# Where the last head's pooling is handed out, which queue loads the padded grids, and where sixteen modulation rows are computed

## The chip, the cores and the metric

The kernel runs on one core of a Trainium2 chip. The metric is the device time of one execution in microseconds (us); of several executions the median is taken. A core has a matrix engine (TensorE, PE in the profile), VectorE (DVE), ScalarE (ACT), GpSimd (POOL) and SyncE (SP), each with an instruction stream of its own; they wait for each other by semaphores. Transfers between device memory and the core's memory (SBUF) are started by an instruction in the stream of SP or POOL and carried by sixteen DMA engines. A load is "handed out" where the program asks for it, and it "lands" when its data is there.

## The reference, cut to what matters

One layer over 512 latent tokens and 256 context tokens of width 1024, in fp32. A combined input projection feeds a pooling mixer and a four-head mLSTM; a gated sum of the two goes through the output projection, and an FFN of width 2816 follows. The layer is modulated by six vectors of 1024 that are computed from `c` (`mod = silu(c) @ w_ada + b_ada`). What the change touches is the pooling mixer and the last four of these six vectors:

```python
mod = jax.nn.silu(c) @ w_ada[l] + b_ada[l]
sh1, sc1, g1, sh2, sc2, g2 = jnp.split(mod[:, None, :], 6, axis=-1)
...
for g, w in enumerate(POOL_WINDOWS):                 # windows 2, 4, 8, 16
    ug = uf[..., g * G:(g + 1) * G]                  # 256 channels of each group
    ug2 = ug.reshape(B, rows, GRID_W, G)             # 8 rows of 64 tokens
    s_r, cnt_r = _window_sum(ug2, w, 1)
    s_rc, cnt_c = _window_sum(s_r, w, 2)
    mean = (s_rc / (cnt_r[:, None] * cnt_c[None, :])[None, :, :, None]).reshape(B, N, G)
    outs.append(jnp.einsum('bnc,cd->bnd', (mean - ug).astype(u.dtype), w_pool[g]))
...
y = jax.nn.sigmoid(p[5]) * pool_out + jax.nn.sigmoid(p[6]) * m_out
return y @ w_out
```

## The kernel before, in words

Channels lie on the 128 partitions, tokens along the free dimension, so a tile of 128 channels by 512 tokens is the unit of work. Every fp32 operand is split into a high and a low part, ACT rounding the high part and DVE subtracting for the low part, and every product is three matmuls (`mm3`, lines 188 to 190: high by high, high by low, low by high). `wload` (L153 to L157) loads a weight strip, ACT makes `wh` (L156), DVE makes `wl` (L157). `split` (L177, L178) does the same for any tile, so `pm` at L177 is the high part and at L178 the low part of a pooled tile, and `act` that of an input of the output projection.

**The stage of pairs.** The pooling input and its gate are projected by a Strassen scheme, eight weight pairs, class `Seven` with the subclass `Pool`. `prepare` loads two strips of a pair (L224 `ur`, L225 `wr`), and makes its sums and splits on ACT and DVE; one low part per strip comes by an accumulating load on POOL's queue (L236, 128 rows of 2 KB; the first of the stage starts at 76.4 us, the last at 149.2 us). `Pool.later` (L852) stores the gate and calls `late_mod(2, ...)`, `Pool.done` stores the pooling input `ud[j]` to device memory.

**Modulation rows.** `late` runs over the 32 blocks of the last four modulation vectors. `late_mod(n, behind, among)` (L676) takes the next `n`: a load of 512 KB (L683) and one DVE instruction (L685) that multiplies by `silu(c)` and sums along the row. Among the pairs the load goes to the `wr` buffers (three, shared with the weight strips), else to the `pb` buffers (two, shared with the pooling). Sixteen are taken among the pairs, two for each pair, and sixteen behind the scores of the attention.

**Heads.** `for h in range(H)` (about L1075): attention of head `h`; queries and keys of head `h+1`; `both_pooled(h)`; `values(h+1)`; and `mixed(h, pp)`, which multiplies the two pooled tiles by `wpool` and combines them with the head's output. `pooled(j)` sets the grid buffer `pa` to zero on POOL (L617), loads `ud[j]` into its middle (L618: 128 partitions, 8 rows of 256 bytes in each, from SP), sums over rows and columns on DVE (L624 or L629, then L634), loads the reciprocal window sizes (L637), multiplies (L641) and subtracts (L642), and splits into `pm`. There is one `pa` buffer: the next tile's zeroing waits for L642 of the tile before. In the last head there are no next keys and values; in their place the six finished tiles of the mixer's output (`yd`) are loaded again by SP (`y_split`, L1048) and split into `act`, and the output projection starts on them. There `rest()` turns the last half of the head's output by transposes (L1013).

Outside two blocks of manual order a list scheduler puts the instructions of each engine in order. It goes by the order in which the program hands them out and by the tiles' dependencies, so a call that is moved in the program moves instructions of other work too.

## Time and profile before

| | |
|---|---|
| time, median of 3 runs (lowest, highest) | 902.58 us (902.25, 903.84) |
| profiled execution, own time | 906.13 us |
| profiled execution, span from first to last instruction | 904.4 us |
| mean granted TensorE clock | 0.992 |
| PE busy | 880.4 us, 97% of the span |
| DVE, ACT, POOL busy | 640.7 us, 474.1 us, 78.9 us |
| DMA, mean over the span | 149 GB/s |

A row of the waits reads: engine, tile and line that waited, "<-" and what ended the wait, then us in total, times, longest. A row of the timeline reads: start, duration, engine, line, operation, tiles, and in brackets how long the engine had been idle before it and what ended that. "xN" are N instructions of a kind put together. A row of the windows gives the busy time of PE, PEld, DVE, ACT and POOL with their instructions, the granted clock, the share of the sixteen DMA engines, and GB/s.

### The profile page before, as it was taken

How to read it: one execution, taken by the hardware profiler on the slowest of the kernel's cores; microseconds unless marked ns; L12 is line 12 of the kernel's file. 1: busy time of each engine (PE TensorE's matmuls, PEld its weight loads, DVE VectorE, ACT ScalarE, POOL GpSimd, SP SyncE). 2: the span in 40 equal slices, each digit the busy share in tenths (PEclk: the TensorE clock that was granted, in tenths of full speed). 3: DMA queues.
4: the chain of work that ended last, by engine and by line, in shares of the span. 5: the costliest groups of instructions: out<-in, count | busy, mean ns of one | idle time of the engine just before them, and what ended most of it. 6: DMA issues, size and time to landing. Idle time of an engine off the chain costs nothing. (4 is left out here: it accounts for less than half of the span.)

```text
span 904.4 us, 15980 instructions
## 1 busy us (share of the span) xinstructions
PE 880.4 (97%) x6218; PEld 810.7 (90%) x6218; DVE 640.7 (71%) x1243; ACT 474.1 (52%) x919; POOL 78.9 (9%) x109
## 2 busy tenths in 40 slices
PE   9999999999999999999999899999999999999997
PEld 8679999879897989989887699999889998899997
DVE  4699896679667867877687667885366754867644
ACT  4576564456536454635364348574145741666542
POOL 0001111000001001100100000020011100111000
PEclk9999999999999999999999899999999999999999
DMA  9838999723126313712436550385356643766402
GB/s 353 307 119 214 281 329 254 266 60 110 55 82 198 107 59 105 223 44 73 150 119 197 196 180 22 81 215 126 93 159 150 146 118 87 203 142 132 127 1 94
DMA packets 56397, 135.12 MB, mean 149 GB/s; under 512 B 13536, under 2 KB 17920, under 8 KB 55296
## 3 DMA queue, kind: packets, MB, share of 16 engines
q1 hardware_dynamic: 48544, 119.93, 40.7%
q0 software_dynamic: 7776, 14.16, 9.5%
q8 instruction: 49, 0.80, 0.4%
q14 instruction: 28, 0.23, 0.1%
HBM read 125.40 MB, written 8.67 MB: 148 GB/s over the span
## 5 line engine op out<-in xcount | busy, mean ns | idle before, releaser
L157 DVE TENSOR_TENSOR wl<-wr,wh 128x1024 fp32r<-128x1024 f32 (+3 forms) x62 | 72.8, 1175 | 34.3 <-ACT wh L156 33.6
L156 ACT CAST wh<-wr 128x1024 fp32r<-128x1024 f32 (+3 forms) x62 | 61.8, 1000 | 64.5 <-PE ps L189 47.2
L188 PE MATMUL ps<-a,wh 128*128 128x512 f32 (+1 forms) x240 | 88.8, 370 | 0.0
L189 PE MATMUL ps<-a,wh 128*128 128x512 f32 (+1 forms) x240 | 88.7, 370 | 0.0
L190 PE MATMUL ps<-a,wl 128*128 128x512 f32 (+1 forms) x240 | 88.6, 369 | 0.0
L188 PE MATMUL ps<-act,wh 128*128 128x512 f32 (+1 forms) x224 | 78.7, 351 | 1.9 <-ACT wh L156 1.8
L190 PE MATMUL ps<-act,wl 128*128 128x512 f32 (+1 forms) x224 | 78.4, 350 | 0.9 <-DVE wl L157 0.9
L189 PE MATMUL ps<-act,wh 128*128 128x512 f32 (+1 forms) x224 | 78.2, 349 | 0.0
L177 ACT CAST wh<-sg 128x1024 fp32r<-128x1024 f32 x27 | 28.4, 1051 | 56.4 <-PE pat L189 46.0
L723 PE MATMUL ps<-wl,a 128*128 128x256 f32 (+1 forms) x192 | 54.4, 284 | 0.9 <-DVE wl L157 0.9
L236 POOL DMA_DIRECT2D ol<-in_wffi x38 | 32.9, 873 | 256.4 <-ACT ol L235 86.9
L722 PE MATMUL ps<-wh,a 128*128 128x256 f32 (+1 forms) x192 | 54.3, 284 | 0.0
L724 PE MATMUL ps<-wh,a 128*128 128x256 f32 (+1 forms) x192 | 54.3, 283 | 0.0
L190 PEld LDWEIGHTS ps<-a,wl 128*128 128x128 f32 x240 | 45.2, 189 | 7.2
L1336 DVE SCALAR_TENSOR_TENSOR x<-ps,lb,x 128x512 f32<-128x512 f32 (+1 forms) x32 | 19.6, 616 | 45.2 <-PE ps L190 45.2
L178 DVE TENSOR_TENSOR wl<-sg,wh 128x1024 fp32r<-128x1024 f32 x27 | 33.0, 1224 | 26.0 <-ACT wh L177 25.8
L189 PEld LDWEIGHTS ps<-a,wh 128*128 128x128 f32 x240 | 45.3, 189 | 6.9
L188 PEld LDWEIGHTS ps<-a,wh 128*128 128x128 f32 x240 | 45.3, 189 | 6.8
L188 PE MATMUL ps<-hp,gh 128*128 128x256 f32 x176 | 50.2, 285 | 1.0 <-ACT pat L272 1.0
L188 PEld LDWEIGHTS ps<-act,wh 128*128 128x128 f32 x224 | 42.7, 191 | 7.9 <-ACT wh L156 2.3
L188 PE MATMUL ps<-hp,oh 128*128 128x256 f32 x176 | 49.2, 279 | 0.1
L190 PE MATMUL ps<-hp,gl 128*128 128x256 f32 x176 | 49.1, 279 | 0.0
(365 smaller groups left out, 3023.4 us busy)
## 6 DMA issues: line engine op xcount, KB each, us to landing
wr<-in_w SPq DMA_DIRECT2D x34, 512.0 KB, 4.7
wr<-in_wffi SPq DMA_DIRECT2D x25, 512.0 KB, 4.2
ur<-in_wffi SPq DMA_DIRECT2D x19, 512.0 KB, 4.2
ol<-in_wffi POOLq DMA_DIRECT2D x38, 256.0 KB, 5.2
ada<-in_wada_a SPq DMA_DIRECT2D x8, 1024.0 KB, 8.7
wr<-in_wada_b SPq DMA_DIRECT2D x16, 512.0 KB, 5.7
pb<-in_wada_b SPq DMA_DIRECT2D x16, 512.0 KB, 4.7
wr<-in_wffo SPq DMA_DIRECT2D x16, 448.0 KB, 3.7
```

Source lines behind the costliest of these rows:

```text
L156: nc.scalar.copy(wh, raw[:, :n])
L157: V.tensor_sub(wl, raw[:, :n], wh.bitcast(F32))
L177: nc.scalar.copy(h, src)
L178: low_part[0] = V.tensor_sub(l, src, h.bitcast(F32))
L188: nc.tensor.matmul(dst, wh, ah, start=first and i == 0, stop=False, skip_group_check=on)
L189: nc.tensor.matmul(dst, wh, al, start=False, stop=False, skip_group_check=on)
L190: nc.tensor.matmul(dst, wl, ah, start=False, stop=last and i == n - 1, skip_group_check=on)
L236: nc.gpsimd.dma_start(l, dram, accum_op=ALU.add)
L722: nc.tensor.matmul(acc[:, :n], ah, wh, start=kk == 0, stop=False)
L723: nc.tensor.matmul(acc[:, :n], ah, wl, start=False, stop=False)
L724: nc.tensor.matmul(acc[:, :n], al, wh, start=False, stop=kk == KT - 1)
L1336: V.scalar_tensor_tensor(x1[j][:, c], acc[:, c], g2[:, j:j + 1], x1[j][:, c], ALU.mult, ALU.add)
```

## The change

Four edits, made together. `pooled` issues the grid load from POOL's stream, right behind its zeroing. The reciprocals are loaded once in `both_pooled(h)` and shared by the head's two tiles, four loads in place of eight. In the last head `both_pooled(h)` is called ahead of the six `y_split(j)`. And `Pool.later` takes one modulation row for an even pair and two for an odd one, 12 in all; the four that are left go to the end of `values(1)` and `values(2)`, which are handed out in the passes of head 0 and head 1, two each, with loads into `pb`.

```diff
--- before.py
+++ after.py
@@ -598,7 +598,7 @@
         return ks
 
 
-    def pooled(j):
+    def pooled(j, ic):
 
         w = (2, 4, 8, 16)[j // 2]
         R, W0 = 8, 64
@@ -615,7 +615,7 @@
         n = R + rl + rr
         A = view(tl("pa", [P, PBW]), n, wid)
         nc.gpsimd.memset(A, 0.0)
-        nc.sync.dma_start(A[:, rl:rl + R, lw:lw + W0], ud[j].rearrange("p (r c) -> p r c", r=R))
+        nc.gpsimd.dma_start(A[:, rl:rl + R, lw:lw + W0], ud[j].rearrange("p (r c) -> p r c", r=R))
         steps = [1] + [2 ** (i + 1) for i in range({2: 0, 4: 1, 8: 2, 16: 3}[w])]
         cur = A
         if w <= 8:
@@ -633,8 +633,6 @@
             B = pb(n, cw - st)
             V.tensor_add(B, cur[:, :, 0:cw - st], cur[:, :, st:cw])
             cur, cw = B, cw - st
-        ic = S("tmp")
-        nc.sync.dma_start(ic, icnt[j // 2:j // 2 + 1, :].broadcast_to([P, T]))
         mean = S("tmp")
         m3 = mean.rearrange("p (r c) -> p r c", r=R)
         i3 = ic.rearrange("p (r c) -> p r c", r=R)
@@ -730,7 +728,9 @@
                 for d, j in ((0, i), (1, 1 - i if i < 2 else 7 - i)):
                     V.tensor_add(gif[:, :, d, j, :], gsrc[:, d], bsrc[:, d])
             nc.scalar.copy(vh[:, i, :DH], acc[:, :DH])
-            V.tensor_sub(vl[:, i, :DH], acc[:, :DH], vh[:, i, :DH].bitcast(F32))
+            low = V.tensor_sub(vl[:, i, :DH], acc[:, :DH], vh[:, i, :DH].bitcast(F32))
+            if 0 < h < H - 1 and i in (0, 1):
+                late_mod(1, low)
         return vh, vl
 
 
@@ -852,7 +852,7 @@
         def later(self, j, s, y, q):
             tanh_half(s[:, TC:], y)
             nc.sync.dma_start(td[j], s)
-            late_mod(2, self.sub, True)
+            late_mod(1 + j % 2, self.sub, True)
 
         def done(self, j, s, x, q):
             nc.scalar.copy(q[:, :TC], x)
@@ -1059,7 +1059,9 @@
         return t
 
     def both_pooled(h):
-        return [pooled(2 * h + e) for e in range(2)]
+        ic = S("tmp")
+        nc.sync.dma_start(ic, icnt[h:h + 1, :].broadcast_to([P, T]))
+        return [pooled(2 * h + e, ic) for e in range(2)]
 
     def mixed(h, pp):
         yb = pool_mix(h, pp)
@@ -1085,9 +1087,9 @@
             for n in ("att", "kqp", "vg"):
                 close_pool(n)
             open_pool("late1", ("act", "oh", "ol", "gh", "gl"))
+            pp = both_pooled(h)
             for j in range(6):
                 y_split(j)
-            pp = both_pooled(h)
             mgate_all(KT - 1)
             rest()
         mixed(h, pp)
```

The places that the prediction speaks of, as the instruction streams stand before and after. The edits shift the line numbers: L681, L639, L640, L651 and L663 after are L683, L641, L642, L653 and L665 before.

**SP in the stage of pairs.** `wr_...<-in_wada_b` is the load of a modulation row, `wr` and `ur` `<-in_w` are the strips of a pair. Before, the loads of the first pairs:

```order
L683 DMA wr_1201<-in_wada_b 128x1024
L224 DMA ur_1236<-in_w 128x1024
L683 DMA wr_1204<-in_wada_b 128x1024
L225 DMA wr_1235<-in_w 128x1024
L854 DMA td<-tmp_1101 128x512
L224 DMA ur_1368<-in_w 128x1024
L859 DMA ud<-tmp_1074 128x512
L683 DMA wr_1333<-in_wada_b 128x1024
L683 DMA wr_1336<-in_wada_b 128x1024
L225 DMA wr_1367<-in_w 128x1024
```

After:

```order
L681 DMA wr_1201<-in_wada_b 128x1024
L224 DMA ur_1233<-in_w 128x1024
L225 DMA wr_1232<-in_w 128x1024
L681 DMA wr_1330<-in_wada_b 128x1024
L854 DMA td<-tmp_1101 128x512
L224 DMA ur_1365<-in_w 128x1024
L859 DMA ud<-tmp_1074 128x512
L681 DMA wr_1333<-in_wada_b 128x1024
L225 DMA wr_1364<-in_w 128x1024
```

Ahead of the strip `wr` of a pair there stood two modulation rows and now there is one.

**POOL at the end of head 0.** `pa` are the grids of head 0's second tile and of head 1's first, L900 are the decay masks of head 1. Before:

```order
L1004 TENSOR_TENSOR rst_2393<-ss_2392,mhalf 128x2
L617 MEMSET pa_3092 128x585
L617 MEMSET pa_4013 128x737
L900 TENSOR_TENSOR tmp_3332<-E_3331,maskF 128x256
L900 TENSOR_TENSOR tmp_3332<-E_3331,maskB 128x256
L900 TENSOR_TENSOR tmp_3427<-E_3426,maskF 128x256
L900 TENSOR_TENSOR tmp_3427<-E_3426,maskB 128x256
```

After:

```order
L1004 TENSOR_TENSOR rst_2381<-ss_2380,mhalf 128x2
L617 MEMSET pa_3080 128x585
L618 DMA pa_3080<-ud 128x8x64
L617 MEMSET pa_4007 128x737
L618 DMA pa_4007<-ud 128x8x64
L900 TENSOR_TENSOR tmp_3324<-E_3323,maskF 128x256
L900 TENSOR_TENSOR tmp_3324<-E_3323,maskB 128x256
L900 TENSOR_TENSOR tmp_3419<-E_3418,maskF 128x256
L900 TENSOR_TENSOR tmp_3419<-E_3418,maskB 128x256
```

Each zeroing now has its load behind it in the same stream, and the masks stand behind both.

**DVE in the last head.** `pa`, `pb`, `pm` belong to the two pooled tiles (grids of 128x316 and smaller), `act` are the low parts of the six loaded tiles, `wl` 128x1024 that of a strip of the output projection. Before:

```order
L178 TENSOR_TENSOR act_5693<-tmp_5690,act_5692 128x512
L641 TENSOR_TENSOR tmp_5721<-pb_5717,tmp_5719 128x512
L178 TENSOR_TENSOR act_5699<-tmp_5696,act_5698 128x512
L642 TENSOR_TENSOR tmp_5721<-tmp_5721,pa_5702 128x512
L157 TENSOR_TENSOR wl_5904<-wr_5901,wh_5903 128x1024
L178 TENSOR_TENSOR pm_5725<-tmp_5721,pm_5724 128x512
L1037 TENSOR_TENSOR m_5335<-m_5335,m_5221 128x512
L629 TENSOR_TENSOR pb_5731<-pa_5728 128x316
L629 TENSOR_TENSOR pb_5733<-pb_5731 128x158
L629 TENSOR_TENSOR pb_5735<-pb_5733 128x79
L634 TENSOR_TENSOR pb_5737<-pb_5735 128x78
L634 TENSOR_TENSOR pb_5739<-pb_5737 128x76
```

After, from the second tile's column sums on:

```order
L634 TENSOR_TENSOR pb_5695<-pb_5693 128x78
L634 TENSOR_TENSOR pb_5697<-pb_5695 128x76
L634 TENSOR_TENSOR pb_5699<-pb_5697 128x72
L634 TENSOR_TENSOR pb_5701<-pb_5699 128x64
L157 TENSOR_TENSOR wl_5896<-wr_5893,wh_5895 128x1024
L639 TENSOR_TENSOR tmp_5703<-pb_5701,tmp_5660 128x512
L1037 TENSOR_TENSOR m_5329<-m_5329,m_5215 128x512
L640 TENSOR_TENSOR tmp_5703<-tmp_5703,pa_5686 128x512
L178 TENSOR_TENSOR pm_5707<-tmp_5703,pm_5706 128x512
L178 TENSOR_TENSOR act_5713<-tmp_5710,act_5712 128x512
L178 TENSOR_TENSOR act_5719<-tmp_5716,act_5718 128x512
L98 SCALAR_TENSOR_TENSOR m_5746<-tmp_5780,m_5746 128x512
```

The splits of `act` stood ahead of both `pm` and around the first; now both `pm` come first, and the strip's `wl` stands between the second tile's column sums and its multiplication.

**ACT in the last head.** The names are the same; `wh` 128x1024 and `gh` are strips of the output projection, L653 (L651 after) scales the pooled product. Before:

```order
L177 CAST act_5698<-tmp_5696 128x512
L156 CAST wh_5903<-wr_5901 128x1024
L177 CAST pm_5724<-tmp_5721 128x512
L1015 ACTIVATE m_5221<-pat_5822,quarter_mg 128x256
L1015 ACTIVATE m_5222<-pat_5822,quarter_mg 128x256
L177 CAST gh_5952<-wr_5950 128x1024
L177 CAST gh_5958<-wr_5956 128x1024
L94 ACTIVATE tmp_5788<-ps_5789 128x512
L177 CAST pm_5750<-tmp_5747 128x512
L653 ACTIVATE tmp_5842<-ps_5835,half_ps 128x512
L653 ACTIVATE tmp_5851<-ps_5844,half_ps 128x512
L156 CAST wh_5928<-wr_5926 128x1024
```

After:

```order
L177 CAST pm_5682<-tmp_5679 128x512
L177 CAST gh_5944<-wr_5942 128x1024
L156 CAST wh_5895<-wr_5893 128x1024
L1015 ACTIVATE m_5215<-pat_5814,quarter_mg 128x256
L1015 ACTIVATE m_5216<-pat_5814,quarter_mg 128x256
L177 CAST pm_5706<-tmp_5703 128x512
L177 CAST act_5712<-tmp_5710 128x512
L177 CAST act_5718<-tmp_5716 128x512
L94 ACTIVATE tmp_5780<-ps_5781 128x512
L177 CAST act_5724<-tmp_5722 128x512
L651 ACTIVATE tmp_5834<-ps_5827,half_ps 128x512
L177 CAST act_5730<-tmp_5728 128x512
```

The high part of the second `pm` stood behind all six of `act` and now stands ahead of them, with a `gh` and the strip's `wh` ahead of it.

## Prediction

> **What bounds the kernel now.** I read the page first, then PE's waits, then the timeline at each longer wait. On the page:
>
> ```profile
> PE 880.4 (97%) x6218; PEld 810.7 (90%) x6218; DVE 640.7 (71%) x1243; ACT 474.1 (52%) x919; POOL 78.9 (9%) x109
> ```
>
> PE is busy for 880.4 of 904.4 us and the change takes no matmul away, so it can only move PE's idle time and its clock. PE's waits:
>
> ```profile
> PE ps L188 <- ACT pm L177: 3.5, 2, 1.9
> PE ps L188 <- ACT pat L272: 3.3, 2, 2.3
> PE ps L190 <- DVE wl L157: 2.9, 5, 1.2
> PE ps L188 <- ACT wh L156: 1.8, 1, 1.8
> ...
> PE ps L189 <- DVE pm L178: 0.6, 1, 0.6
> ```
>
> Rows one, four and five lie in the last head and make 5.9 us. The first row's 3.5 us are waits for `pm`, the pooled tiles. The longest wait of the second row lies in the stage of pairs. The third row is spread over the ends of the heads. The clock is shown by two windows of 10 us:
>
> ```profile
> 490.00:500.00 10.00, 6.54 (x28) 4.72 (x26) 8.08 (x17) 5.01 (x8) 0.62 (x1) 1.00 0.54 177
> 500.00:510.00 10.00, 7.61 (x23) 5.68 (x23) 6.80 (x10) 4.56 (x7) 0.00 (x0) 0.66 0.34 99
> ```
>
> Right behind the waits of the last head the granted clock is 0.66 over 10 us: 10 x (1 - 0.66) = 3.4 us of streaming lost, or 6.8 us at half speed.
>
> **Part 1, four modulation rows leave the pairs.** SP, DVE, ACT and PE there:
>
> ```profile
> 100.00 1.31 SPq L683 DMA_DIRECT2D wr<-in_wada_b  x2
> 102.76 0.33 SPq L225 DMA_DIRECT2D wr<-in_w  x1
> ...
> 105.72 1.22 DVE L685 SCALAR_TENSOR_TENSOR wr<-wr,crow_s 128x1024 f32<-128x1024 f32 x1 [2.71 <-DMA wr<-in_wada_b]
> ...
> 109.55 0.62 ACT L231 CAST oh<-wr 128x512 fp32r<-128x512 f32 x1 [1.98 <-DMA wr<-in_w]
> ...
> 114.04 0.38 PE L188 MATMUL ps<-hg,gh 128*128 128x256 f32 x1 [2.32 <-ACT pat L272]
> ```
>
> And the window around it:
>
> ```profile
> 105.00:115.00 10.00, 7.68 (x66) 7.48 (x66) 9.25 (x14) 5.98 (x12) 1.75 (x2) 1.00 1.03 310
> ```
>
> The strip of L225 is handed out behind two rows of 512 KB while the DMA engines are full (share 1.03, 310 GB/s); ACT waits 1.98 us for it, and through ACT's copy of `pat` PE waits 2.32 us. With one row ahead in place of two the strip moves up by 512 KB / 310 GB/s = 1.7 us, and its buffer, one of three, comes free one DVE instruction (1.22 us) earlier. I take 2.0 of the 2.32 us as gone, bounds 1.0 and 2.3.
>
> The four rows come back in heads 0 and 1, two each: 2 x 1.22 us of DVE a head, and two loads into `pb`, which the pooling rotates through too. They stand between the `wl` of the head's end. There DVE had idle time:
>
> ```profile
> 278.11 1.23 DVE L157 TENSOR_TENSOR wl<-wr,wh 128x1024 fp32r<-128x1024 f32 x1 [1.83 <-ACT wh L156]
> ...
> 362.82 1.23 DVE L157 TENSOR_TENSOR wl<-wr,wh 128x1024 fp32r<-128x1024 f32 x1 [1.08 <-ACT wh L156]
> ```
>
> 1.83 and 1.08 us cover part of 2.44 us each; 0.6 and 1.4 us are left, 2.0 together, and DVE's work for the next head's decays queues behind them. Between nothing, if PE has other work meanwhile, and 4.9 us, if none is covered, I take +1.5 us, near the 2.0.
>
> **Part 2, the grid load on POOL's queue.** How it goes from SP, in SP's waits, in the answer for its line, and on the timelines of SP and DVE:
>
> ```profile
> SPq L618 <- POOL pa L617: 23.1, 6, 6.6
> ```
>
> ```profile
> L618 SPq DMA_DIRECT2D pa<-ud x8: 529/534/619, 173.9 to 491.8; - x8
> ...
> DMA to landing us min/median/max: 3.1/3.7/5.9
> ```
>
> ```profile
> 265.32 0.54 SPq L618 DMA_DIRECT2D pa<-ud  x1
> ...
> 268.99 0.70 DVE L624 TENSOR_TENSOR pb<-pa 128x520 f32<-128x520 f32 x1 [2.68 <-DMA pa<-ud]
> ...
> 353.42 0.42 DVE L733 TENSOR_TENSOR vl<-ps,vh 128x256 fp32r<-128x256 f32 x1 [1.98 <-ACT vh L732]
> ...
> 433.64 0.53 SPq L618 DMA_DIRECT2D pa<-ud  x1
> ...
> 436.95 1.20 DVE L624 TENSOR_TENSOR pb<-pa 128x994 f32<-128x994 f32 x1 [1.21 <-DMA pa<-ud]
> ...
> 491.78 0.53 SPq L618 DMA_DIRECT2D pa<-ud  x1
> ...
> 494.97 0.49 DVE L629 TENSOR_TENSOR pb<-pa 128x316 f32<-128x316 f32 x1 [1.61 <-DMA pa<-ud]
> ```
>
> The second tile of a head cannot be loaded before the first has left the one buffer, so its load is waited for by DVE in heads 0, 2 and 3 (the rows above), and whatever the load takes longer is on the path of `pm`. SP's 23.1 us of waiting for the zeroing go, but what is queued behind it there lands early enough, so I cost that at nothing. The only loads on POOL's queue in the trace are the accumulating ones:
>
> ```profile
> L236 POOL DMA_DIRECT2D ol<-in_wffi x38: 862/862/1219, 582.9 to 840.7; - x38
> ...
> DMA to landing us min/median/max: 3.9/5.4/9.1
> ```
>
> They have 128 rows of 2 KB; the grid has 1,024 rows of 256 bytes, and no row shows that on POOL. Bounds: 3.1 us, the fastest grid load from SP, and 9.1 us, the slowest on POOL's queue. The DMA engines are about half idle at these places, as in the quiet landings, and the grid load doesn't read back what it writes, so I take the quiet end, 3.9 us. From SP these second tiles were there 268.99 - 265.32 = 3.7, 436.95 - 433.64 = 3.3 and 494.97 - 491.78 = 3.2 us after their issue, 3.4 in the mean, so 0.5 us more each. In head 1 DVE idles for another reason (row 353.42) and turns to the grid right after, so I count it in full: heads 0 to 2 cost 3 x 0.5 = +1.5 us. The last head's load is counted below.
>
> The Trainium skill ("DMA: Bandwidth & Descriptors", section "Latency and other measured facts") gives a first byte after about 0.6 us from SP's kind of queue and about 1 us from GpSimd's. By that the three heads would cost 3 x 0.4 = 1.2 us in place of 1.5, and the sum would be 0.3 us lower.
>
> **Part 3, one load of reciprocals a head.** The first tile's multiplication still waits for it as now, the second finds it there. Nothing, except at the last head (below).
>
> **Part 4, the last head.** Before:
>
> ```profile
> 482.39 0.70 POOL L1004 TENSOR_TENSOR rst<-ss,mhalf 128x2 f32<-128x2 f32 x1 [14.14 <-DVE ss L1003]
> ...
> 484.57 1.29 DVE L178 TENSOR_TENSOR act<-tmp,act 128x512 fp32r<-128x512 f32 x2 [2.26 <-ACT act L177]
> ...
> 489.12 0.69 DVE L641 TENSOR_TENSOR tmp<-pb,tmp 128x512 f32<-128x512 f32 x1 [0.51 <-DMA tmp<-in_icnt]
> ...
> 489.50 1.05 ACT L156 CAST wh<-wr 128x1024 fp32r<-128x1024 f32 x1 [0.93 <-PE ps L189]
> ...
> 489.54 0.60 PE L1013 MATMUL pat<-ident,tmp 128*128 128x128 f32 x4
> ...
> 491.13 0.62 POOL L617 MEMSET pa<- 128x632 f32 x1 [8.04 <-issue]
> ...
> 497.93 0.69 DVE L642 TENSOR_TENSOR tmp<-tmp,pa 128x512 f32<-128x512 f32 x1
> ...
> 498.66 0.62 ACT L177 CAST pm<-tmp 128x512 fp32r<-128x512 f32 x1 [0.25 <-DVE tmp L642]
> ...
> 499.33 0.73 PE L188 MATMUL ps<-pm,wh 128*128 128x512 f32 x2 [1.86 <-ACT pm L177]
> ...
> 503.70 0.79 PE L188 MATMUL ps<-act,wh 128*128 128x512 f32 x1 [1.84 <-ACT wh L156]
> ```
>
> L641 of the first tile waits for reciprocals that SP issues behind six `yd` loads, though DVE was done with the sums by 484.57 - 2.26 = 482.3. After, with the reciprocals handed out ahead of the `yd` loads, L641 and L642 (0.69 each) follow there and end at 483.7. POOL's zeroing starts there (its L1004 is done at 483.1), ends at 484.3, and the load lands at 484.3 + 3.9 = 488.2. From there L629 and L634 take what they took before, 494.97 to 497.21, so 2.2 us: 490.4. Now the strip's `wl` stands next, and waits for `wh`, which ACT can't start before PE leaves its buffer at 489.5 and which takes 1.05; with a `gh` ahead of it on ACT I take 490.9 for its end. Then 1.2 for `wl` (row 278.11) and three times 0.69 for L641, L1037 and L642: 494.2, and ACT's `pm` (0.62) is there at 494.8.
>
> PE ends the four transposes at 490.1 and has the first tile's six matmuls (6.54 / 28 = 0.23 us each, by the first window) until 491.5, so it waits 3.3 us once, where it waited 1.59, 1.86 and 0.55 us. The matmuls that follow go at the pace of DVE's low parts: `pm`, five of the six `act`, L98 and L1037, eight of 0.65 us (row 484.57, two in 1.29), 5.2 us, and some 0.8 us for the last products and the next strip, an estimate from 0.23 us a matmul: 500.8. ACT's `wh` for the next strip is now queued between `act` and not behind the last `pm`, so the 1.84 us wait goes. PE stands at 500.8 where it stood at 503.7: -2.9 us.
>
> **The clock.** The 6.8 us at half clock before lost 3.4 us. One wait of 3.3 us instead of three takes up less time; I take one spell of half that length, -1.7 us, bounds 0 and -3.4.
>
> By the Trainium skill ("TensorE: Matmul & The Clock Gate", Part 1) the clock falls after an idle window of about 3.4 us. In the trace it fell at a row where PE had worked between waits of under 2 us, so the trace does not bear out that a whole window must be idle; by the page's rule nothing would fall at 3.3 us, and the sum would be 1.7 us lower.
>
> **The sum.** -2.0 (pairs) + 1.5 (rows in heads 0 and 1) + 1.5 (loads in heads 0 to 2) - 2.9 (last head) - 1.7 (clock) = -3.6 us against the profiled execution: 902.5 us own time for 906.13 us (904.4 of span and 1.7 outside it). The median of the runs shown is 3.55 us below that execution, so 902.58 - 3.6 = 899.0 us.
>
> **The rivals.**
>
> *GpSimd pays by the row (slower).* Place: L618 on POOL. If all of the 862 ns for 128 rows grows with the rows, 1,024 rows take 6.9 us; if half is fixed, 3.9 us. Each us of later landing is paid in heads 0 to 2 and in the last, so four times: 899.0 + 4d for a landing that is d later than my 3.9 us. It decides from d = 0.9 (a landing of 4.8 us); d = 2 gives 907.0; with half fixed d = 3.9 - 0.9 = 3.0 and 911.0, with none fixed d = 6.0 and 923.0. For it: 1,024 rows are eight times any load on this queue, and landings there reach 9.1 us. Against: it is not known that any of the 862 ns grows, and the landing is made up of other parts too. Chance 0.32.
>
> *VectorE holds GpSimd up.* Here POOL's load would stretch while DVE works. Place: L618 beside DVE's adds. Price from the row: the slowest issue is 1,219 ns beside a median of 862, so 0.36 us a load, 4 x 0.36 = +1.4: 900.4. Against: the least and the median issue are both 862 ns though DVE is busy 71% of the time. The Trainium skill ("SBUF — State Buffer", the "DVE blocks DMA" box) warns of this for a DMA from GpSimd's queue and advises another queue; by these rows only its mild form is likely. It is part of the forecast's range, chance 0.1.
>
> *No change.* The order moves, but the second `pm` gates the last head as before, or the rows in heads 0 and 1 eat up what the pairs gain (+4.9 in place of +1.5: -0.2 us), 902.4. For it: the one `pa` buffer stays. Chance 0.13.
>
> **How the numbers follow.** Forecast 0.45 at 899.0 (895.5 to 901, from the bounds of the pairs, the rows and the clock), the VectorE rival 0.1, no change 0.13, pay by the row 0.32, a third of it with d over 3. About 0.2% (1.8 us) is what a measurement of this kernel can tell from no change. Faster: 0.45 + 0.1 = 0.55. Same: 0.13. Slower: 0.32. The range is 896 to 911, up to the half-fixed case: below it some 0.06, above it 0.11.
>
> **What would show it.** POOL's L618 near 0.9 us with landings near 3.9 us; DVE's waits for `pa` in heads 0 to 2 about 0.6 us longer; the 2.32 us wait for `pat` at 114 us under 1 us; one wait for `pm` of about 3.3 us in the last head, none for `wh`; a window behind it with a clock above 0.8. Wrong are the numbers if L618 takes 2 us or more on POOL or its landings pass 5 us, if PE waits longer for `wl` at the ends of heads 0 and 1, or if the clock drops there.

## The result and the profile after

The changed kernel took 911.02 us, the median of 4 runs (909.95 to 911.80), beside 903.21 us for the kernel before on the same chip (4 runs, 902.25 to 905.47): a ratio of 1.0082 with a 95% interval of 1.0059 to 1.0105. It is slower by about 7.4 us, where 899.0 was forecast.

The profiled execution took 909.95 us of its own time with a span of 908.2 us, clock 0.990. Against the profiled execution of before that is 3.8 us more, where the medians differ by 7.8: the execution shown of before lay 2.9 us above the median of its four runs, the one shown after 1.1 us below its own. So the traces speak for 3.8 of the 7.8 us, and where the rest arises they don't show. The page:

```profile
PE 881.1 (97%) x6218; PEld 811.6 (89%) x6218; DVE 643.9 (71%) x1243; ACT 473.3 (52%) x919; POOL 88.6 (10%) x117
```

PE's work is what it was. POOL has the eight issues as well. PE's waits after:

```profile
PE pat L986 <- POOL tmp L900: 5.4, 3, 2.3
PE ps L188 <- ACT pm L177: 4.3, 2, 4.0
...
PE ps L188 <- ACT pat L272: 2.1, 2, 1.1
```

The waits for `pm` are one long one, as forecast, and one of 0.3 us; those for `pat` have shrunk. The first row is new: before, PE waited 0.4 us in all for L900. L900 is POOL's masking of the decays `E` at the start of each head's attention, and no term of the prediction was about PE's wait for it. The new waits stand at three places, and on PE's timeline after they are:

```profile
287.92 0.36 PE L986 MATMUL pat<-vh,Sp 128*128 128x258 f32 x1 [1.54 <-POOL tmp L900]
...
374.77 0.42 PE L986 MATMUL pat<-vh,Sp 128*128 128x258 f32 x1 [2.26 <-POOL tmp L900]
...
464.09 0.36 PE L986 MATMUL pat<-vh,Sp 128*128 128x258 f32 x1 [1.62 <-POOL tmp L900]
...
497.56 0.60 PE L1013 MATMUL pat<-ident,tmp 128*128 128x128 f32 x4
```

The same four matmuls before (the last of them, at 489.54, is in the prediction):

```profile
287.26 0.36 PE L986 MATMUL pat<-vh,Sp 128*128 128x258 f32 x1 [0.36 <-POOL tmp L900]
...
371.49 0.28 PE L986 MATMUL pat<-vh,Sp 128*128 128x258 f32 x1
...
454.97 0.36 PE L986 MATMUL pat<-vh,Sp 128*128 128x258 f32 x1
```

Read down the two: PE is 0.7 us late at the end of head 0, 3.3 us at the end of head 1, 9.1 us at the end of head 2 and 8.0 us at the transposes of the last head. At the end of the span it is 3.8 us late. So the last head gave back 4.2 us, and the loss was made in heads 0 to 2, most of it between 288 and 464 us: 2.6 us more up to the matmul in head 1, some 3.4 us by the clock behind it (below), and the other 2.4 us up to the matmul in head 2, with the third wait of 1.62 us in it.

What stands behind the wait of 2.26 us is seen on the timeline of SP and POOL in head 1, after (`td` and `rd` are the stored gates and the decays that the next head's scores need):

```profile
362.93 0.33 SPq L681 DMA_DIRECT2D pb<-in_wada_b  x1
363.31 0.90 SPq L1058 DMA_DIRECT2D tmp<-td  x2
366.31 0.33 SPq L681 DMA_DIRECT2D pb<-in_wada_b  x1
366.69 0.43 SPq L896 DMA_DIRECT2D E<-rd  x1
...
373.90 0.73 POOL L900 TENSOR_TENSOR tmp<-E,maskF 128x256 f32<-128x256 f32 x1 [8.72 <-DMA E<-rd]
```

And before:

```profile
360.31 1.22 SPq L1058 DMA_DIRECT2D tmp<-td  x2
...
362.14 0.52 SPq L896 DMA_DIRECT2D E<-rd  x1
...
369.86 0.74 POOL L900 TENSOR_TENSOR tmp<-E,maskF 128x256 f32<-128x256 f32 x1 [7.51 <-DMA E<-rd]
```

`E` was asked for 4.5 us later and the mask began 4.0 us later. From the issue to the mask it is 7.2 us after and 7.7 before, so the load itself was not slower: it was handed out late. In SP's stream one more modulation row now stands ahead of `td` and another between `td` and `E`. What these rows waited for, in SP's waits from 357 to 367 us, after:

```profile
SPq L681 <- DVE pb L683: 4.4, 2, 2.4
```

Before, SP has no such wait there. Here a row's load waits until DVE (L683) is done with an earlier row in the same `pb` buffer, and what stands behind it on SP is handed out after it.

The clock, in the windows after:

```profile
375.00:385.00 10.00, 9.49 (x55) 9.20 (x55) 8.43 (x21) 6.24 (x16) 0.32 (x1) 0.66 0.58 164
...
500.00:510.00 10.00, 6.46 (x21) 5.08 (x22) 9.06 (x14) 7.64 (x14) 0.00 (x0) 0.83 0.50 170
```

Before, the window from 375 to 385 us had a clock of 1.00. Behind the new wait in head 1 it is 0.66, which is 10 x 0.34 = 3.4 us of streaming lost. Behind the wait in the last head it is 0.83, half of the loss before, as forecast. In head 0 the window from 285 to 295 us is at 0.83 in both kernels.

The stage of pairs, and the grid loads on POOL:

```profile
113.34 0.38 PE L188 MATMUL ps<-hg,gh 128*128 128x256 f32 x1 [1.14 <-ACT pat L272]
```

```profile
L618 POOL DMA_DIRECT2D pa<-ud x8: 882/923/956, 154.9 to 492.8; - x8
...
DMA to landing us min/median/max: 3.6/3.9/6.7
```

PE's wait for `pat` went from 2.32 to 1.14 us. An issue of the grid takes POOL 0.92 us, and the median landing is 3.9 us, the value that the prediction took. The last head:

```profile
492.76 0.92 POOL L618 DMA_DIRECT2D pa<-ud  x1 [0.30 <-POOL pa L617]
...
496.61 0.49 DVE L629 TENSOR_TENSOR pb<-pa 128x316 f32<-128x316 f32 x1 [1.82 <-DMA pa<-ud]
...
497.77 1.05 ACT L177 CAST gh<-wr 128x1024 fp32r<-128x1024 f32 x1 [3.71 <-DMA wr<-in_wout]
498.73 1.04 ACT L156 CAST wh<-wr 128x1024 fp32r<-128x1024 f32 x1
...
503.54 0.73 PE L188 MATMUL ps<-pm,wh 128*128 128x512 f32 x2 [4.00 <-ACT pm L177]
```

PE has one wait for `pm`, 4.00 us, and none for `wh` behind it.

### The profile page after: what moved, and what is told of

It reads as the page before. It is cut to its first block, busy times and chain, and to the rows that moved or that the text cites. A ratio compares the mean times of both kernels' runs of the same rounds, so it can differ in the third digit from the quotient of the medians.

```text
span 908.2 us, 15981 instructions
## 1 busy us (share of the span) xinstructions
PE 881.1 (97%) x6218; PEld 811.6 (89%) x6218; DVE 643.9 (71%) x1243; ACT 473.3 (52%) x919; POOL 88.6 (10%) x117
## 4 chain that ended last, share of the span: by engine, by line
PE 63%; issue 16%; DVE 9%; DMA 7%; ACT 4%; POOL 1%; SPq 0%; DVEq 0%; POOLq 0%; ACTq 0%
PE ps L188 14%; PE ps L190 14%; PE ps L189 14%; PE pat L189 3%; PE pat L188 3%; PE pat L190 3%; PE pat L490 2%; PE pat L988 2%; PE pat L986 2%; PE pat L987 2%; DMA E<-rd 2%; DVE wl L157 2%; DMA pa<-ud 1%; PE ps L490 1%; PE ps L400 1%
## 5 line engine op out<-in xcount | busy, mean ns | idle before, releaser
L189 PE MATMUL ps<-a,wh 128*128 128x512 f32 (+1 forms) x240 | 88.6, 369 | 0.0
L190 PE MATMUL ps<-a,wl 128*128 128x512 f32 (+1 forms) x240 | 88.6, 369 | 0.0
L188 PE MATMUL ps<-hp,gh 128*128 128x256 f32 x176 | 50.2, 285 | 1.0 <-ACT pat L272 1.0
L189 PE MATMUL ps<-hp,gh 128*128 128x256 f32 x176 | 48.9, 278 | 0.0
```

Source lines behind the costliest of these rows:

```text
L188: nc.tensor.matmul(dst, wh, ah, start=first and i == 0, stop=False, skip_group_check=on)
L189: nc.tensor.matmul(dst, wh, al, start=False, stop=False, skip_group_check=on)
L190: nc.tensor.matmul(dst, wl, ah, start=False, stop=last and i == n - 1, skip_group_check=on)
```

## The experiments

Theory at this point: in the heads, what costs is the order on SP's queue (rows ahead of `td` and `E`), and the grid load's landing. Rivals: the rows cost through DVE's time; GpSimd pays for the grid by the row; the orders that the scheduler derives anew cost more than any single operation. A ratio is always to the kernel before on the same chip, whose median there was 905.0 to 905.6 us, so 0.001 is 0.9 us. Each kernel's timeline and waits come from one of its executions, which spread by 4 to 13 us in the kernels shown here; they show where time goes, and the ratio shows how much.

**Each edit alone.** Four kernels, each the kernel before with one of the four edits of the diff.

The rows:

```diff
+            low = V.tensor_sub(vl[:, i, :DH], acc[:, :DH], vh[:, i, :DH].bitcast(F32))
+            if 0 < h < H - 1 and i in (0, 1):
+                late_mod(1, low)
...
-            late_mod(2, self.sub, True)
+            late_mod(1 + j % 2, self.sub, True)
```

> The kernel before with the modulation-row edit alone (12 rows among the pairs, two each at the end of values(1) and values(2)). Theory A (the rows): their loads hold SP's queue at the ends of heads 0 and 1 until a pb buffer is free, the load of the next head's decays (E<-rd) behind them is late, GpSimd's masks L900 follow late and PE waits for them; the pairs give 1.4 us back. Expected +3 to +6 us against before, with a wait of PE for L900 over 1.5 us in heads 1 or 2 and E<-rd issued some 4 us later than before in head 1. Theory B (the queue) and theory C (the shared reciprocals): this edit alone is worth the pairs, -1.4 us, between -2 and +1, and PE's waits for L900 stay near 0.4 us.

Measured: 1.0062 [1.0037, 1.0086], +5.6 us. SP and POOL in head 1, and PE's wait (the edit moves L900 to L902):

```profile
361.77 0.33 SPq L683 DMA_DIRECT2D pb<-in_wada_b  x1
362.15 0.90 SPq L1060 DMA_DIRECT2D tmp<-td  x2
364.06 0.33 SPq L683 DMA_DIRECT2D pb<-in_wada_b  x1
364.43 0.43 SPq L898 DMA_DIRECT2D E<-rd  x1
...
372.00 0.72 POOL L902 TENSOR_TENSOR tmp<-E,maskF 128x256 f32<-128x256 f32 x1 [11.35 <-DMA E<-rd]
```

```profile
PE pat L988 <- POOL tmp L902: 3.5, 2, 1.9
```

With the grids loaded from SP as before, rows stand ahead of `td` and `E` here too, `E` is handed out 2.3 us later, the masks are late and PE waits for them. The span shown is 1.8 us longer than that of before (906.2 and 904.4 us), so this trace has a third of the 5.6 us in it.

The queue:

```diff
-        nc.sync.dma_start(A[:, rl:rl + R, lw:lw + W0], ...
+        nc.gpsimd.dma_start(A[:, rl:rl + R, lw:lw + W0], ...
```

> The kernel before with the grid load alone moved to GpSimd's stream. Theory B (the queue): the masks L900 stand behind the load on GpSimd, so they are late and PE waits for them; each second pooled tile is 0.5 us later besides: +4 to +8 us against before, with over 3 us of PE waits for L900. Theory A and theory C: only the later landings cost, 0.3 to 0.6 us in each of four heads, so +1 to +2.5 us, and PE's waits for L900 stay under 1.5 us in sum.

Measured: 1.0082 [1.0056, 1.0109], +7.4 us. The last head on the timeline and PE's longest waits:

```profile
493.62 0.92 POOL L618 DMA_DIRECT2D pa<-ud  x1 [0.30 <-POOL pa L617]
493.80 0.33 SPq L153 DMA_DIRECT2D wr<-in_wout  x1
...
498.99 0.49 DVE L629 TENSOR_TENSOR pb<-pa 128x316 f32<-128x316 f32 x1 [4.02 <-DMA pa<-ud]
```

```profile
PE ps L188 <- ACT pm L177: 7.5, 3, 4.9
```

The issue is 0.92 us for 1,024 rows, beside 0.86 us for 128 on the same queue, so GpSimd does not pay by the row. But from issue to first use this grid took 498.99 - 493.62 = 5.4 us, where it took 3.2 from SP. SP's order before:

```profile
491.78 0.53 SPq L618 DMA_DIRECT2D pa<-ud  x1
492.41 0.61 SPq L153 DMA_DIRECT2D wr<-in_wout  x1
```

There the strip of 512 KB stood behind the grid. Now it is handed out by 494.13 us, while GpSimd is still busy with the grid's issue (493.62 to 494.54). PE's waits for `pm` went from 3.5 to 7.5 us. The masks, which stand behind the grid on POOL, cost PE 0.7 us, so the time is as the theory of the queue expected, but not by the wait that it named.

The reciprocals, once per head:

> The kernel before with the reciprocals loaded once per head. Theory C (the shared reciprocals): the one tile is held until the second tile's multiplication, the small tiles rotate differently, and the masks of the next head get their buffer late: +2 to +5 us against before, with PE waits for L900 over 1.5 us. Theory A and theory B: within 1 us of before, L900 waits near 0.4 us.

Measured: 1.0019 [0.9993, 1.0046]: no effect that can be told from none.

The order of the last head:

```diff
+            pp = both_pooled(h)
             for j in range(6):
                 y_split(j)
-            pp = both_pooled(h)
```

> The kernel before with the last head's pooling handed out ahead of the six loads, and nothing else. All theories expect the gain of the last head here: one wait for pm in place of two and no wait for wh, with half as much time at half clock, -3 to -5 us against before. A rival (the last head's gain needs the other edits, above all the reciprocals that are loaded early): -1 us or less.

Measured: 0.9942 [0.9917, 0.9968], -5.2 us. ACT and PE in its last head:

```profile
489.67 1.05 ACT L156 CAST wh<-wr 128x1024 fp32r<-128x1024 f32 x1 [3.57 <-PE ps L189]
...
491.35 1.04 ACT L177 CAST gh<-wr 128x1024 fp32r<-128x1024 f32 x1
...
494.48 0.79 PE L188 MATMUL ps<-pm,wh 128*128 128x512 f32 x1 [2.80 <-ACT pm L177]
```

Here `wh` stands ahead of `gh` on ACT; in the changed kernel it is the other way round (497.77 and 498.73 there), and PE's wait is 2.80 us in place of 4.00.

The four alone add up to 5.6 + 7.4 + 1.7 - 5.2 = +9.5 us, together they cost +7.4.

**One edit undone in the changed kernel.** The same diffs, taken back one at a time.

> The changed kernel with the grid load back on SP; the other three edits stay. By the edits alone, added up (order -5.2, rows +5.6, reciprocals +1.7): +2 us against before. If the queue's price lies only in the last head as it was ordered before, where GpSimd's grid load lost its place ahead of a strip of the output projection, it is small once the pooling comes first, and this stays near the changed kernel: +6 to +8 us.

Measured: 0.9999 [0.9979, 1.0018]. Its PE waits:

```profile
PE pat L986 <- POOL tmp L900: 3.6, 2, 2.1
PE ps L188 <- ACT pm L177: 2.8, 1, 2.8
```

> The changed kernel with the modulation rows back among the pairs. By the edits alone, added up (order -5.2, queue +7.4, reciprocals +1.7): +4 us against before. If the waits of PE for the masks L900 in the changed kernel (5.4 us in sum) and the clock that falls behind them come from the rows: those waits under 1.5 us and no fall of the clock in head 1, and the time -2 to +1 us against before.

Measured: 1.0016 [0.9992, 1.0041].

> The changed kernel with the six loads of the last head handed out ahead of the pooling again. By the edits alone, added up (rows +5.6, queue +7.4, reciprocals +1.7): +14 us against before. If the gain of the order is the same with the other edits beside it, this is 5 us above the changed kernel, +12 to +13 us; if the order only hides the queue's price in the last head, more than that.

Measured: 1.0106 [1.0081, 1.0131].

So in the changed kernel the queue is worth 7.4 us, the rows 6 us and the order -2.2 us, the last too little to stand clear of the two intervals. Taking the grid loads back to SP brings `pm`'s wait to 2.80 us, the value of the order alone, and leaves waits for the masks, which the rows alone make as well. With the rows taken back 1.9 us in two waits for the masks are left (5.4 in three before), in heads 1 and 2, so not all of these waits are the rows'. The order brings less in the company of the other edits than alone (-2.2 against -5.2).

**Where the queue's price lies.** The kernel before with the last head's two grids on GpSimd, then the order with those two, then the order with the other six:

```diff
-        nc.sync.dma_start(A[:, rl:rl + R, lw:lw + W0], ...
+        (nc.gpsimd if j >= 6 else nc.sync).dma_start(A[:, rl:rl + R, lw:lw + W0], ...
```

> The kernel before with the grid load on GpSimd for the last head's two tiles alone. If the queue's price lies in the last head (there the second grid took 5.4 us from issue to DVE's start in place of 3.2, beside a strip's load): +2.5 to +7 us against before, nearly all of the edit for all heads. If it is paid once in each head: a quarter, +1.5 to +2 us.

Measured: 1.0061 [1.0040, 1.0082], +5.5 of the 7.4 us.

> The last head's order with the grid load of its two tiles on GpSimd, the others on SP. If the price of the queue in the last head as ordered before (+5.5 us) came from the strip that SP issued beside the second grid, there is none beside it here: the grid takes 3.8 us in place of 3.4, PE's wait for pm grows by about 0.5 us, and the time is 0.5 to 2 us above the order alone, -3 to -5 us against before. If GpSimd's queue has its price by itself: 5 us above the order alone, -1 to +1 us.

Measured: 0.9986 [0.9967, 1.0004], -1.3 us, which is 4 us above the order alone. The second grid with SP's next strip, then ACT and PE:

```profile
482.83 0.94 POOL L618 DMA_DIRECT2D pa<-ud  x1 [0.30 <-POOL pa L617]
483.87 0.33 SPq L153 DMA_DIRECT2D wr<-in_wout  x1
...
486.59 0.49 DVE L629 TENSOR_TENSOR pb<-pa 128x316 f32<-128x316 f32 x1 [1.75 <-DMA pa<-ud]
```

```profile
487.99 1.05 ACT L177 CAST gh<-wr 128x1024 fp32r<-128x1024 f32 x1 [3.88 <-DMA wr<-in_wout]
488.95 1.04 ACT L156 CAST wh<-wr 128x1024 fp32r<-128x1024 f32 x1
...
493.76 0.79 PE L188 MATMUL ps<-pm,wh 128*128 128x512 f32 x1 [3.83 <-ACT pm L177]
```

The strip is handed out right behind the grid's issue here, and from issue to first use the grid takes 3.8 us; so it does in the changed kernel (492.76 to 496.61). It took 5.3 to 5.4 us where the strip was handed out within 0.2 us of the start of the grid's issue: with the queue alone, with the last two grids alone, and in the changed kernel without the order. So the strip goes with the late landing, but most of the price stays without it, against the expectation that goes by the strip. What is seen in its place: with two loads on another queue `gh` and `wh` are turned round on ACT, PE waits 3.83 us in place of 2.80, and the clock's loss doubles: the window from 490 to 500 us is at 0.66 here and at 0.83 with the order alone.

> The last head's order with the grid loads of heads 0 to 2 on GpSimd and those of the last head on SP. The last head's share is known from the run of the order with its two loads on GpSimd (+4 us above the order alone). If the queue's price is nearly all in the last head: -5 to -4 us against before, as the order alone. If heads 0 to 2 pay as well (each second grid 0.4 us later, and td and E<-rd beside the grid of the next head): +2 to +4 us above the order alone, -3 to -1 us against before.

Measured: 1.0057 [1.0036, 1.0078], +5.2 us, which is 10 us above the order alone and against the expectation. Its timeline and PE's waits:

```profile
487.64 0.86 SPq L637 DMA_DIRECT2D tmp<-in_icnt  x2
...
491.62 0.69 DVE L641 TENSOR_TENSOR tmp<-pb,tmp 128x512 f32<-128x512 f32 x1 [1.77 <-DMA tmp<-in_icnt]
```

```profile
PE ps L188 <- ACT pm L177: 5.6, 2, 5.4
```

In the last head, whose grids come from SP here, it lost by its reciprocals: they were issued at 487.64 us, behind a strip, where the order alone issues them at 474.63, of which 7 us are a delay that the whole kernel has there (the transposes begin at 496.64 in place of 489.70). The first multiplication waits for them, the zeroing and the second grid come behind it, and PE waits 5.4 us.

But of the 11.7 us between the two spans (910.4 and 898.7) 7.7 are lost by the matmul behind the masks in head 2, and 5.1 of these between heads 1 and 2. The same stretch of PE's timeline, from the matmul behind the masks in head 1 to the one in head 2:

| kernel | head 1 | head 2 | between |
|---|---|---|---|
| before | 371.49 | 454.97 | 83.5 us |
| order alone | 370.66 | 455.31 | 84.7 us |
| queue alone | 371.36 | 457.02 | 85.7 us |
| changed, order undone | 371.69 | 457.12 | 85.4 us |
| changed, queue undone | 374.29 | 459.04 | 84.8 us |
| order, first six grids on POOL | 373.24 | 462.98 | 89.7 us |
| changed, rows undone | 373.83 | 462.46 | 88.6 us |
| changed | 374.77 | 464.09 | 89.3 us |

The last three have both the first six grids on POOL and the last head's order, and they take 3 to 5 us more than the four with one of the two. In the changed kernel 4.6 of the 5.8 us between its span and that with the queue undone (908.2 and 902.4) lie in this stretch: 1.62 us is the wait for the masks in head 2, which is not there with the queue undone, and 1.7 us is the clock, which fell to 0.66 behind the wait in head 1 and to 0.83 with the queue undone. So the two edits cost together what neither costs alone, in heads that the order edit does not name; that the scheduler, which derives all orders anew, makes this is argued and not shown, and which instruction's place it is was not followed up.

**What of the rows costs.** First the rows among the pairs 12 as in the change, but the four placed behind the scores, where such rows stood already:

```diff
-            late_mod(2, self.sub, True)
+            late_mod(1 + j % 2, self.sub, True)
...
-            late_mod(2, low_part[0])
+            late_mod(2 + (h < 2), low_part[0])
```

> 12 modulation rows among the pairs, and the four left not in values but behind the scores of heads 0 and 1, three in place of two at each of four places. The place decides (the rows in values stand on SP ahead of E<-rd, these stand behind it): -2 to +1 us against before, PE's waits for the masks near 0.4 us. Any place in the heads costs, since the rows take DMA and VectorE there: +3 to +6 us, as in values.

Measured: 0.9968 [0.9945, 0.9991], -2.9 us. SP in head 1:

```profile
357.69 1.14 SPq L1058 DMA_DIRECT2D tmp<-td  x2
...
359.52 0.49 SPq L896 DMA_DIRECT2D E<-rd  x1
```

No modulation row stands between `td` and `E`, and PE has no wait for L900. The same four rows of work at another place: +5.6 becomes -2.9.

Then the rows as in the change, with `E` loaded by GpSimd's queue:

```diff
-            nc.sync.dma_start(sa.rearrange("p (d j t) -> p d j t", d=2, j=2),
+            nc.gpsimd.dma_start(sa.rearrange("p (d j t) -> p d j t", d=2, j=2),
```

> The modulation-row edit alone, as in the run of the rows, with one thing more: the loads of the decays (E<-rd) are issued by GpSimd in place of SP, so that the moved rows' loads on SP no longer stand ahead of them. If the rows cost because they hold SP ahead of E<-rd: E<-rd is issued before 363 us in head 1, the waits of PE for the masks shrink from 3.5 us to under 1.5 us, and the time falls from +5.6 us to between -2 and +2 us against before. If they cost by VectorE's 2.4 us a head or by the full DMA engines: the waits of PE at the head's start stay, +4 to +7 us.

Measured: 1.0099 [1.0071, 1.0128], +9.0 us, more than either theory expected, so it does not decide. `td`, which the scores need as well, stayed on SP behind the rows; that this is the reason is not shown, since only the times are used here.

Then the rows' parts apart. Without the four loads (four blocks of the modulation are not computed, here and in the run after it):

```diff
+            row = crow_s
+            if not bare:
+                nc.sync.dma_start(wa[:, :D], wada_b[i])
+                row = wa[:, :D]
```

> The modulation-row edit alone, with the loads of the four moved rows left out: their VectorE instruction reads silu(c) twice and still writes a pb buffer, so these four blocks of the modulation are not computed. Theory hold (the moved rows take both pb buffers, so the loads of the next rows behind the scores, which stand on SP ahead of td and E<-rd, wait on SP until VectorE frees a buffer): the buffers are taken as before, so +3 to +6 us against before and waits of PE for the masks over 1.5 us. Theory traffic (1 MB more through the DMA engines at the head's end makes td and E<-rd late): -2 to +1 us.

Measured: 0.9970 [0.9952, 0.9987], -2.7 us. This goes against the theory of the hold as expected above (+3 to +6), and lies just under the range of the theory of the traffic (-2 to +1). `E` and its mask in head 1:

```profile
364.30 0.44 SPq L901 DMA_DIRECT2D E<-rd  x1
...
370.06 0.73 POOL L905 TENSOR_TENSOR tmp<-E,maskF 128x256 f32<-128x256 f32 x1 [11.04 <-DMA E<-rd]
```

`E` is handed out as late as with the loads (364.43), now behind strips, but the mask begins 5.8 us after that and not 7.6, and PE's waits for the masks are 0.7 us and not 3.5. So a late issue of `E` does not make the loss by itself. And without the loads and without the `pb` buffer, DVE's work alone, in two halves:

```diff
+            if bare:
+                wa = S("tmp")
+                with tc.issue_after(behind.ins):
+                    for c in (0, T):
+                        V.scalar_tensor_tensor(wa, crow_s[:, c:c + T], 0.5, crow_s[:, c:c + T], ALU.mult, ALU.mult,
+                                               accum_out=mods[:, i:i + 1])
+                continue
```

> The same with the loads left out and the VectorE work written to a small tile in two halves, so that no pb buffer is taken (these four blocks of the modulation are not computed). Theory hold: the loads behind the scores go out early, as in the kernel before; what is left is VectorE's 2.5 us in heads 0 and 1 and the gain of the pairs, -2 to +2 us against before, masks waited for under 1 us. Theory VectorE (the work itself delays the next head): +4 to +7 us.

Measured: 1.0016 [1.0000, 1.0032], +1.5 us. With DVE's four instructions there and the loads gone the edit gains as much as with the rows behind the scores, so DVE's time is not what costs, and the kernels with and without the loads differ by 5.6 + 2.7 = 8.3 us. The last kernel lies 4.2 us above the one without loads though it does no more on DVE; it takes a `tmp` buffer in place of `pb`, `E` is handed out at 367.54, and PE waits up to 1.8 us for the masks again. I take that as the size of what a changed order and another buffer do by themselves, so the 8.3 us may have some 4 us of that in them.

**The parts that gain, together.** The order with the rows behind the scores, then also the shared reciprocals:

> The last head's order alone (-5.2 us) with the rows of the run before this one. If the place of the rows decides: -5 to -7 us against before, the fastest of all. If any place in the heads costs: -2 to +1 us.

Measured: 0.9912 [0.9886, 0.9939], -8.0 us, a median of 897.74 us, the fastest of all.

> The fastest kernel so far (the order, and the four rows behind the scores, -8.0 us against before) with the reciprocals loaded once a head as well. If the shared reciprocals cost nothing or 1.7 us, as the run of that edit alone leaves open: -8 to -6 us against before. If they save SP and the DMA engines something: under -9 us.

Measured: 0.9932 [0.9912, 0.9953], -6.2 us: the shared reciprocals bring nothing. The two gains add up (5.2 + 2.9 = 8.1), and PE's waits have none for the masks in them.

## Why the prediction was wrong

**The sum, term by term.** Between the pairs and the transposes of the last head the prediction had -2.0 + 1.5 + 1.5 = +1.0 us; the trace has +8.0. Behind that it had -2.9 - 1.7 = -4.6; the trace has 3.8 - 8.0 = -4.2. So in the execution shown the last head came out about as worked out, and what failed are the two terms of +1.5 us for heads 0 to 2: by the ratios of the runs the rows cost about 8 us and the loads on POOL 7.4.

**The pairs (-2.0): the right mechanism, a smaller size.** The wait shrank by 1.18 us, near the lower bound of 1.0. With the four rows at a harmless place the whole edit gives -2.9 us, so the 2.0 lies between what the wait and the ratio say.

**The rows (+1.5): this step failed.** It counted what each row does on DVE, 2.44 us a head against 1.83 and 1.08 us of idle time. Without the loads that part cost nothing that shows (-2.7 in all, against -2.9 at the harmless place). What it did not count are the two loads a head as instructions on SP, at a place where `td` and `E` of the next head stand behind them. The order of SP's queue at that place does not appear in the prediction, only DVE's. At this place the edit costs 5.6 us and at the other it gains 2.9, so the place of the rows is worth about 8 us, and that is shown. How the loads do it stays open. For the holding of the queue speak the 2.3 us by which `E` was issued later in the kernel with the rows alone (364.43 against 362.14), while its way from issue to mask was no longer (7.6 against 7.7 us), and SP's waits for `pb` (4.4 us in the changed kernel). Against it speaks the kernel without the loads, where `E` was issued as late (364.30), its way to the mask was 5.8 us, and nothing was lost; that rather speaks for the bytes beside `td` and `E`. But there the scheduler also placed other loads differently, so the two are not separated.

**The loads on POOL (+1.5): this step failed in what it counted, not in its durations.** The landing is 3.9 us in the median, as taken, and the rival that GpSimd pays by the row falls: 0.92 us for 1,024 rows. Its price of 907 to 911 us was near by accident. VectorE did not hold the issues up either: all eight lie between 0.88 and 0.96 us. The edit costs 7.4 us all the same, alone and in the changed kernel, and not at the same place. With the last head ordered as before, the price is in the last head (5.5 of the 7.4 us with its two grids alone): SP's next strip is no longer behind the grid but handed out beside it, and the grid takes 5.4 us (that the strip slows it is argued from six kernels, and no run took it away alone). That "what is queued behind it there lands early enough, so I cost that at nothing" looked at who waits for the strips and not at whom the strips delay. In the changed kernel the grid of the last head takes 3.8 us, and by the traces four fifths of the price lie between heads 1 and 2, where the last head's order and the queue meet (the table above). Two more things raise it. Other instructions change places (`gh` ahead of `wh`, worth about 1 us of PE's wait, 3.83 against 2.80), and the clock lost more than the wait that it fell behind (3.4 us behind 2.26 us in head 1). The step put all of this at nothing. Which order makes the loss between heads 1 and 2 stays open: no kernel was tried that moves the queue with every order kept.

**The last head (-2.9) and its clock (-1.7): the mechanism right, the size near in the trace.** From the transposes on the changed kernel gained 4.2 us in the execution shown, against 4.6. The ratios don't bear that out as well: the order alone gives -5.2 us, but the forecast has the last head's loads on POOL in it, and the order with those two loads gives -1.3. One wait for `pm` of 4.00 us stands in place of three (3.3 forecast), the wait for `wh` is gone, and the window behind it is at 0.83 in place of 0.66. Less the shift of 8.02 us the grid is there at 488.6 us (488.2 forecast), and PE goes on at 495.5 (494.8).

**The clock in the heads** had no term at all. "If the clock drops there" stood under what would make it wrong, at the ends of heads 0 and 1. It dropped in head 1, for 3.4 us, behind the wait for the masks and not for `wl`.

**The range.** Its upper side does not follow from the bounds that it names: with 1.0 us from the pairs, 4.9 for the rows and nothing from the clock the sum comes to 905.1 us and not 901. That is still 6 us under what was measured.

**The reciprocals (nothing): right** within the measurement.

**The chances.** Slower had 0.32, all of it for the wrong mechanism. The rivals that should have been there are loads queued ahead of others on SP, in this place, and orders that the scheduler derives anew.

## What to carry to other kernels

When a step is moved, write down its loads with the queue's rows ahead and behind, as for its arithmetic: here the place of four loads was worth about 8 us where the arithmetic was worth nothing. A load that goes to another queue no longer keeps the loads behind it back, so look for what now runs beside it. Where a scheduler derives the order, an edit of a queue alone may turn others' instructions round, so time each edit by itself and taken back from the whole: of the four here one gained 5.2 us alone and 2.2 in company, one gains 2.9 at another place, one did nothing and one cost 7.4. And compare positions along the whole timeline, since a loss can lie in another stage than the edit.

## What the runs showed of the hardware

GpSimd's issue hardly depended on the number of rows: 0.92 us for 1,024 rows of 256 bytes, 0.86 for 128 rows of 2 KB. Between the end of its own zeroing and the issue 0.30 us went by. In the changed kernel the landing was 3.6 us at the quickest. From issue to first use the second grid of the last head took 5.3 to 5.4 us in the three kernels where SP handed out a strip within 0.2 us of the issue's start, and 3.8 to 3.9 us in three where the strip came 1.0 us after it.

The clock fell behind short waits, and not each time: a wait of 2.80 us in the kernel with the order alone left a window at 0.83, that is 1.7 us lost; one of 2.26 us in head 1 of the changed kernel left one at 0.66, 3.4 us lost; one of 1.62 us in its head 2 left the clock at 1.00. In head 0 of the kernel before three waits of 0.36, 0.64 and 0.42 us within 3 us left the window from 285 to 295 us at 0.83. The Trainium skill ("TensorE: Matmul & The Clock Gate", Part 1), as the prediction cited it, wants an idle window of about 3.4 us for that. These runs don't bear that out: no wait at these places was as long.
